# Where low parts of weights are made, and when convolution taps are queued, in a two-layer diffusion block on one Trainium2 core

## The chip, the cores and the metric

The kernel runs on one core of one Trainium2 chip. The core has TensorE (PE, matrix products; PEld is its weight load), VectorE (DVE), ScalarE (ACT), GpSimd (POOL) and SyncE (SP, which here only issues DMAs), and 16 DMA engines that move data between the chip's memory (HBM) and the core's on-chip memory (SBUF). The metric is the device time of one execution in microseconds (us); lower is better. Before the change three runs took 3119.43, 3118.53 and 3109.94 us, median 3118.53 us.

## The reference, cut to what matters

All arithmetic is float32: 1024 latent tokens and 256 context tokens, width 1024, two layers.

```python
for l in range(DEPTH):                                    # DEPTH = 2
    sh1, sc1, g1, sh2, sc2, g2 = split(silu(c) @ w_mod[l] + b_mod[l], 6)    # c_ctx likewise
    h = rms_norm(x, norm1_g[l]) * (1 + sc1) + sh1
    q, k, v, u_pool, a, b = split(h @ w_in[l])            # 4 heads, v 128 wide
    attn = softmax(q1 k1) - lam * softmax(q2 k2), times v, then rms_norm   # over ctx + latent
    pool = windows of 2, 4, 8, 16 tokens, then a 64x64 product
    conv = silu(layer_norm(depthwise_conv_31_taps(a * sigmoid(b))))
    x = x + g1 * (concat(attn, pool, conv) @ w_out[l])
    x = x + g2 * swiglu(rms_norm(x, norm2_g[l]) * (1 + sc2) + sh2)         # hidden width 2816
    # in layer 0 the context tokens pass through the same steps; they see context alone
```

## The kernel before, in words

TensorE multiplies in a rounded float32 format (fp32r). To keep accuracy each operand is held as two tiles, a high part `hi` (the value rounded) and a low part `lo` (the value less `hi`), and each product is three matmuls, hi·hi, hi·lo and lo·hi. Activations live transposed, 128 channels on the partitions, in two latent blocks of 512 tokens and one context block of 256.

Weights are read tile by tile by the class `Stream`. `load_to` issues the load of a raw tile on SP's queue; `split_to` makes `hi` with an ACT copy and `lo` in one of three ways, by a letter in the tuple `lo`, which is gone through in turn: "v" is a subtraction on VectorE, "p" the same on GpSimd, and "d" is an ACT copy of minus `hi` followed by a DMA issued from GpSimd's queue that reads the same weights from HBM once more and adds them onto it (an adding DMA). `get(i)` splits up to `split_ahead` tiles beyond tile i and loads `raw_ahead` more. `ahead(raw, split)` first splits up to `split` tiles and then loads up to `raw`; where `split_to` finds a tile that is not loaded, it issues the load and the ACT copy right behind it. Raw, hi and lo tiles of 512 KB, residual tiles, attention results and many temporaries all come from one pool of 23 slots, called `big`; smaller ones from `half` and `part`. An instruction that writes a tile waits until the slot is free, and every engine and queue runs its instructions in the order in which they were written out.

That order is written by a planner in the program itself. The class `Clock` keeps a modelled time for each engine. Work off TensorE's main line is cut into steps, Python generators in named lanes, and `adv`, called after each group of matmuls, issues steps whose due time is not past the modelled time of PE. A step that ends with `yield "v"` is due one us before VectorE's modelled queue runs out; one that ends with `yield "v-"`, used by the convolution's taps alone (`taps`, one VectorE instruction for each tap), is due 0.3 us after it has run out.

The stages of a layer, with the profile's times:

- Opening (0 to 85 us): the first two modulation parts, the first norm.
- `in_proj` (85 to 371 us in layer 0, 1835 to 2062 us in layer 1): columns of w_in, then v's four weight tiles (w_v). Beside it run the taps (lanes conv0, conv1, and convc for the context in layer 0), the layer norm behind them (`conv_end`), the pooling and the norms of q and k. In layer 0 lane "ada" computes the third modulation part (g1) from 16 tiles of 256 KB, with `lo` by adding DMAs.
- `attention` (371 to 636 us with eight context units ahead; 2062 to 2265 us): all engines in a hand-made order; what is left of taps and `conv_end` is put between.
- `out_proj` for the two latent blocks (636 to 755 us, 2265 to 2385 us), eight steps of 24 matmuls for each block, then for the context (755 to 802 us, layer 0). In layer 0 lane "ada" computes the next modulation parts beside it with VectorE products (`adaln_v`), which the second norm needs.
- The feed-forward part (from 814 and 2385 us on), whose weights get their low part on GpSimd.

Of the kernel before, what the change touches and what calls it, by code (L numbers as in the profile page):

```python
# [17 lines left out]
KD = D // P  # L18
# [47 lines left out]
QK_LANES = 2  # L66
ADA_AT = 25.0
GATED = 4
V_AHEAD = {2: (1, 1), 1: (3, 2), 0: (4, 4)}
CTX_LO = ("v", "p", "p")  # L70
EARLY = 3
POOL_ENG = "v"

# [123 lines left out]
class Kern:  # L197
# [20 lines left out]

    def due(self, name):
        d = self.lanes[name][0]  # L220
        return self.clock.at[d[0]] + (0.3 if d.endswith("-") else -1.0) if isinstance(d, str) else d

    def _step(self, name):
        q = self.lanes[name]
# [39 lines left out]
    def finish(self, *names):  # L264

        while True:
            due = [(self.due(n), n) for n in (names or list(self.lanes)) if n in self.lanes]
            if not due:
                return
            if "ada" in self.lanes and any(n.startswith("norm") for _, n in due):  # L270
                due.append((self.due("ada"), "ada"))
            self._step(min(due)[1])
# [323 lines left out]
    def in_proj(self, l, st, lat, cxb, soon, opened=None):  # L596
# [53 lines left out]
        for j in range(GATED, len(COLS)):  # L650
# [4 lines left out]
            w = st.get(j, 2)  # L655
            if len(COLS) - j - 1 in V_AHEAD:
                sv.ahead(*V_AHEAD[len(COLS) - j - 1])
            outs = [self.bank() for _ in blocks]
# [476 lines left out]


    def out_stream(self, l, n, **kw):
        return Stream(self, [self.io["w_out"][l, d] for _ in range(n) for d in range(KD)], **{"raw_ahead": 1, **kw})

    def out_proj(self, st, blocks, ready, xs, x_load, gate, done, soon=None):  # L1140

# [154 lines left out]
    def run(self):  # L1296
# [161 lines left out]
        self.lane("norm1", self.norm_h([x[1] for x in xs], rs[1], scale, shift, lat[1]))  # L1458
        self.lane("norm2", norm_c())
        self.lane("small", self.lambdas(), 60.0)  # L1460
        self.lane("ada", self.adaln(0, [2], 3.0, ne=1, split_ahead=2, raw_ahead=1, lo=("d",)), ADA_AT)

        for l in range(DEPTH):
            last = l == DEPTH - 1
# [95 lines left out]
            def ctx_soon():  # L1560
                st_out.append(self.out_stream(l, 1, raw_ahead=2, split_ahead=2, lo=CTX_LO))
                st_out[1].ahead(3, 2)
# [227 lines left out]
```

## Time and profile before

| | us | share |
|---|---|---|
| profiled execution, device time | 3113.99 | |
| its span, first to last instruction | 3112.2 | |
| PE busy | 2923.8 | 94% |
| DVE busy | 1723.9 | 55% |
| ACT busy | 1076.2 | 35% |
| POOL busy | 838.0 | 27% |
| DMA, mean | 97 GB/s | |
| granted TensorE clock, mean | 0.973 of full | |

A busy PE is not PE at its peak, since matmuls are pipelined and the granted clock varies; the shares are averages over stages with different limits, so what a stage is limited by is read from that stage's own rows.

### The profile page before, as it was taken

The page shows a single profiled execution, that of the slowest core. Times are in us where ns is not written, and L with a number is a line of the kernel's source. Part 1 is how long each engine was busy: PE and PEld are TensorE (multiplying, and loading weights), DVE is VectorE, ACT ScalarE, POOL GpSimd, SP SyncE. Part 2 cuts the span into 40 slices and gives each one's busy share as a digit, 9 for nine tenths or more (in the row PEclk, how much of TensorE's full clock was granted, in tenths as well). Part 3 has the DMA queues.
Part 4 walks back from the last instruction along what each step waited for, and adds up shares of the span by engine and source line. Part 5 has one row for each costly group of instructions (what it writes and reads, how often), then busy time and mean ns, then how long its engine had stood idle before and what let it go on. Part 6 is the DMA issues. An engine that isn't in the chain of part 4 may idle for free.

```text
span 3112.2 us, 37712 instructions
## 1 busy us (share of the span) xinstructions
PE 2923.8 (94%) x14572; PEld 2406.1 (77%) x14572; DVE 1723.9 (55%) x2674; ACT 1076.2 (35%) x1851; POOL 838.0 (27%) x759
## 2 busy tenths in 40 slices
PE   7799978988799999999999979989999999999999
PEld 3587767876688888888888768878877888888887
DVE  5777788967845554444332478769955222322223
ACT  4554367733422222221222234457734111111110
POOL 0110057810223232333322100038811222112121
PEclk9899989999899999999999989999999999999999
DMA  6565642265222222221111224672252111111111
GB/s 218 138 153 135 199 145 76 86 236 201 92 80 70 74 82 81 69 81 48 41 35 34 83 81 116 166 220 62 89 183 71 52 48 48 48 48 48 48 48 54
DMA packets 143618, 302.37 MB, mean 97 GB/s; under 512 B 14544, under 2 KB 56144, under 8 KB 143440
## 3 DMA queue, kind: packets, MB, share of 16 engines
q1 hardware_dynamic: 137104, 281.09, 28.3%
q0 software_dynamic: 6336, 18.88, 3.6%
q8 instruction: 115, 1.88, 0.2%
q14 instruction: 63, 0.52, 0.1%
HBM read 250.63 MB, written 49.28 MB: 96 GB/s over the span
## 4 chain that ended last, share of the span: by engine, by line
PE 62%; DVE 8%; ACT 3%; issue 3%; DMA 2%; POOL 1%; SPq 0%; ACTq 0%; DVEq 0%; POOLq 0%
PE bank L275 60%; DVE half L163 3%; DVE big L163 2%; DVE st L163 2%; ACT half L163 1%; PE S L275 1%; DVE at L163 1%; DMA half<-in_w_mod 1%; PE bank L280 1%; DVE part L163 1%; ACT p L163 1%; ACT big L163 1%; DMA part<-MS 0%; POOL p L163 0%; ACT at L163 0%
## 5 line engine op out<-in xcount | busy, mean ns | idle before, releaser
L275 PE MATMUL bank<-part,big 128*128 128x512 f32 (+1 forms) x7536 | 1621.0, 374 | 55.1 <-DVE part L163 16.3
L275 PEld LDWEIGHTS bank<-part,big 128*128 128x128 f32 x7536 | 1317.5, 191 | 329.0 <-DVE part L163 20.7
L163 POOL TENSOR_TENSOR big<-big,big 128x1024 fp32r<-128x1024 f32 x137 | 333.0, 2447 | 1106.3 <-ACT big L163 821.3
L275 PE MATMUL bank<-half,big 128*128 128x512 f32 (+1 forms) x2640 | 573.2, 375 | 17.3 <-DVE big L163 7.1
L275 PEld LDWEIGHTS bank<-half,big 128*128 128x128 f32 x2640 | 462.9, 190 | 120.8 <-ACT half L163 14.8
L163 DVE TENSOR_TENSOR big<-big,bank 128x512 f32<-128x512 f32 (+1 forms) x130 | 83.1, 679 | 828.4 <-PE bank L275 618.2
L163 DVE SCALAR_TENSOR_TENSOR big<-bank,mod,big 128x512 f32<-128x512 f32 (+1 forms) x560 | 391.1, 737 | 135.2 <-PE bank L275 131.2
L163 ACT ACTIVATE big<-bank 128x512 f32<-128x512 f32 x88 | 48.1, 596 | 659.7 <-PE bank L275 659.6
L163 ACT CAST big<-big 128x1024 fp32r<-128x1024 f32 (+2 forms) x274 | 250.3, 937 | 44.0 <-DVE big L163 19.5
L163 POOL TENSOR_TENSOR p<-p,p 128x512 f32<-128x512 f32 (+1 forms) x200 | 221.4, 1107 | 16.7
L163 ACT ACTIVATE half<-bank,mod 128x256 f32<-128x256 f32 x160 | 76.0, 475 | 426.1 <-PE bank L275 405.7
L163 POOL TENSOR_TENSOR big<-big,half 128x256 f32<-128x256 f32 x160 | 122.5, 766 | 352.0 <-ACT half L163 352.0
L163 DVE TENSOR_REDUCE st<-S 128x1 f32<-128x1280 f32 (+1 forms) x144 | 195.9, 1363 | 10.7 <-PE S L275 10.7
L163 ACT ACTIVATE p<-S,st 128x1280 f32<-128x1280 f32 (+1 forms) x144 | 177.8, 1234 | 44.5 <-DVE st L163 40.4
L163 POOL TENSOR_SCALAR p<-p,st 128x512 f32<-128x512 f32 (+1 forms) x200 | 124.3, 622 | 241.9 <-DVE st L163 182.0
L275 PE MATMUL S<-kv,big 128*128 128x512 f32 (+1 forms) x672 | 157.3, 370 | 10.5 <-ACT p L163 9.7
L275 PEld LDWEIGHTS S<-kv,big 128*128 128x128 f32 x672 | 120.3, 191 | 37.2 <-ACT p L163 15.8
L163 DVE SCALAR_TENSOR_TENSOR big<-big,dww,big 128x1009 f32<-128x1009 f32 (+14 forms) x120 | 148.8, 1272 | 0.4
L163 DVE TENSOR_TENSOR big<-big,big 128x512 fp32r<-128x512 f32 (+4 forms) x141 | 123.8, 886 | 32.5 <-ACT big L163 31.0
L275 PE MATMUL bank<-at,kv 128*128 128x256 f32 x960 | 137.7, 290 | 0.0
L163 DVE TENSOR_TENSOR at<-bank,at 128x512 fp32r<-128x512 f32 (+1 forms) x200 | 115.8, 589 | 28.7 <-ACT at L163 24.9
L163 ACT CAST at<-bank 128x512 fp32r<-128x512 f32 (+1 forms) x200 | 99.6, 508 | 74.7 <-PE bank L280 74.3
(111 smaller groups left out, 2376.9 us busy)
## 6 DMA issues: line engine op xcount, KB each, us to landing
big<-in_w_ffn_in SPq DMA_DIRECT2D x88, 512.0 KB, 3.6
big<-in_w_mod SPq DMA_DIRECT2D x48, 512.0 KB, 3.7
big<-in_w_ffn_out SPq DMA_DIRECT2D x44, 512.0 KB, 3.5
big<-in_w_out SPq DMA_DIRECT2D x40, 512.0 KB, 5.6
half<-in_w_mod SPq DMA_DIRECT2D x64, 256.0 KB, 5.5
big<-QS SPq DMA_DIRECT2D x128, 128.0 KB, 4.7
big<-in_w_in SPq DMA_DIRECT2D x28, 512.0 KB, 4.7
big<-in_w_in POOLq DMA_DIRECT2D x20, 512.0 KB, 5.5
```

The source lines that it names most:

```text
L163: r = fn(*a, **k)
L275: self.tc.nc.tensor.matmul(out, lhsT, rhs, start=start, stop=stop)
L280: self.tc.nc.tensor.transpose(out, in_, ident)
```

## The change

Five edits. The taps become due 0.6 us before VectorE's modelled queue runs out, instead of 0.3 us after. Ahead of the last but one column of w_in, v's third weight tile is split too. The context output projection makes all low parts by adding DMAs, where it went through VectorE, GpSimd, GpSimd in turn. The latent output projections of both layers make theirs by adding DMAs, split two tiles ahead, where VectorE made them one tile ahead. The third modulation part makes its low parts on VectorE, one tile ahead, where adding DMAs made them, two ahead.

```diff
-V_AHEAD = {2: (1, 1), 1: (3, 2), 0: (4, 4)}
-CTX_LO = ("v", "p", "p")
+V_AHEAD = {2: (1, 1), 1: (3, 3), 0: (4, 4)}
+CTX_LO = ("d",)
...
     def due(self, name):
         d = self.lanes[name][0]
-        return self.clock.at[d[0]] + (0.3 if d.endswith("-") else -1.0) if isinstance(d, str) else d
+        return self.clock.at[d[0]] - (0.6 if d.endswith("-") else 1.0) if isinstance(d, str) else d
...
     def out_stream(self, l, n, **kw):
-        return Stream(self, [self.io["w_out"][l, d] for _ in range(n) for d in range(KD)], **{"raw_ahead": 1, **kw})
+        return Stream(self, [self.io["w_out"][l, d] for _ in range(n) for d in range(KD)], **{"raw_ahead": 1, "split_ahead": 2, "lo": ("d",), **kw})
...
-        self.lane("ada", self.adaln(0, [2], 3.0, ne=1, split_ahead=2, raw_ahead=1, lo=("d",)), ADA_AT)
+        self.lane("ada", self.adaln(0, [2], 3.0, ne=1, split_ahead=1, raw_ahead=1), ADA_AT)
```

The default of `lo` in `Stream` is ("v",). Of the context projection's eight low parts three were VectorE's and five GpSimd's.

## Rows read from the trace of the kernel before

**Rows 1.** The page: the span, busy time of PE, and the chain of waits by engine.

```profile
span 3112.2 us, 37712 instructions
...
PE 2923.8 (94%) x14572; PEld 2406.1 (77%) x14572; DVE 1723.9 (55%) x2674; ACT 1076.2 (35%) x1851; POOL 838.0 (27%) x759
...
PE 62%; DVE 8%; ACT 3%; issue 3%; DMA 2%; POOL 1%; SPq 0%; ACTq 0%; DVEq 0%; POOLq 0%
```

**Rows 2.** Busy time by stage: start and end, length, busy us of PE, PEld, DVE, ACT and POOL (with instructions), granted TensorE clock, DMA share, GB/s.

```profile
85.00:185.00 100.00, 84.64 (x409) 65.26 (x408) 74.65 (x112) 52.49 (x89) 18.47 (x25) 0.88 0.67 162
...
371.00:412.00 41.00, 26.49 (x108) 21.81 (x108) 25.18 (x71) 26.04 (x65) 8.82 (x14) 0.67 0.78 235
412.00:490.00 78.00, 58.11 (x352) 49.49 (x351) 67.63 (x117) 50.46 (x94) 48.31 (x56) 0.93 0.32 95
490.00:636.00 146.00, 136.85 (x934) 121.07 (x933) 133.66 (x205) 109.24 (x197) 119.96 (x138) 1.00 0.27 80
636.00:755.00 119.00, 104.53 (x468) 81.58 (x466) 81.13 (x123) 35.93 (x50) 2.67 (x1) 0.96 0.69 243
755.00:802.00 47.00, 39.99 (x257) 37.10 (x256) 41.42 (x57) 17.71 (x27) 12.91 (x5) 0.89 0.43 140
802.00:850.00 48.00, 32.06 (x156) 25.56 (x156) 40.21 (x67) 21.30 (x33) 8.56 (x4) 0.86 0.29 94
...
2265.00:2327.00 62.00, 58.56 (x281) 47.59 (x282) 28.98 (x40) 20.11 (x29) 2.67 (x3) 1.00 0.65 223
2327.00:2385.00 58.00, 58.00 (x259) 46.93 (x257) 40.00 (x56) 26.52 (x37) 7.27 (x3) 1.00 0.24 79
```

**Rows 3.** Waits of PE between 85 and 185 us: waiting engine, line, tile, what it waited for, us in total, times, longest.

```profile
PE mod L275 <- DMA half<-in_w_mod: 11.6, 7, 5.2
PE bank L275 <- DMA big<-in_w_in: 3.5, 1, 3.5
```

**Rows 4.** DMA issues between 100 and 180 us: tiles, queue, count, size, median us from issue to landing.

```profile
half<-in_w_mod POOLq DMA_DIRECT2D x16, 256.0 KB, 8.5
```

**Rows 5.** Groups between 660 and 850 us, shapes kept apart: engine, operation, tiles, shape, count, busy us, mean ns, idle before. The first is the subtraction for a `half` tile, the next two those for a `big` one on GpSimd and on VectorE.

```profile
L163 DVE TENSOR_TENSOR half<-big,half 128x512 fp32r<-128x512 f32 x2 | 1.4, 690 | 0.0
...
L163 POOL TENSOR_TENSOR big<-big,big 128x1024 fp32r<-128x1024 f32 x10 | 26.5, 2660 | 193.7 <-ACT big L163 146.2 <-DVE half L163 39.3 <-PE bank L275 8.2
L163 DVE TENSOR_TENSOR big<-big,big 128x1024 fp32r<-128x1024 f32 x16 | 19.5, 1224 | 5.9 <-ACT big L163 5.9
```

**Rows 6.** Instructions that read the tap weights: count, shortest, median and longest ns, first and last start.

```profile
L163 DVE SCALAR_TENSOR_TENSOR big<-big,dww,big x120: 1259/1272/1286, 98.8 to 2030.1; 128x1009 f32<-128x1009 f32 x8, 128x1010 f32<-128x1010 f32 x8, 128x1011 f32<-128x1011 f32 x8, 128x1012 f32<-128x1012 f32 x8
L163 DVE SCALAR_TENSOR_TENSOR big<-big,dww x60: 460/473/971, 126.4 to 452.0; 128x241 f32<-128x241 f32 x4, 128x242 f32<-128x242 f32 x4, 128x243 f32<-128x243 f32 x4, 128x244 f32<-128x244 f32 x4
```

**Rows 7.** Timeline of VectorE and ScalarE around the start of layer 0's attention: start, length, engine, line, operation, tiles, shape, count. The first is layer 0's last latent tap, the next a silu of `conv_end`, the third two of the last context taps.

```profile
354.14 1.27 DVE L163 SCALAR_TENSOR_TENSOR big<-big,dww,big 128x1009 f32<-128x1009 f32 x1
...
402.99 0.81 ACT L163 ACTIVATE big<-big,params 128x512 f32<-128x512 f32 x1
...
451.51 0.97 DVE L163 SCALAR_TENSOR_TENSOR big<-big,dww 128x242 f32<-128x242 f32 x2
```

**Rows 8.** Timeline of SP, ScalarE and PE at the end of the columns of layer 0; in brackets the idle time before and what ended it.

```profile
295.06 0.33 SPq L163 DMA_DIRECT2D big<-in_w_v  x1
...
301.78 1.04 ACT L163 CAST big<-big 128x1024 fp32r<-128x1024 f32 x1 [7.73 <-DMA big<-in_w_v]
...
304.26 1.26 PE L275 MATMUL bank<-big,pwr 128*128 128x256 f32 x3 [7.27 <-ACT big L163]
```

**Rows 9.** Waits of PE between 660 and 850 us, columns as in rows 3.

```profile
PE bank L275 <- DVE part L163: 15.8, 7, 12.3
PE bank L275 <- ACT big L163: 9.9, 5, 6.5
PE bank L275 <- POOL big L163: 6.1, 3, 2.2
```

**Rows 10.** Timeline of VectorE and GpSimd in that stretch: the same four VectorE products without and beside a GpSimd subtraction.

```profile
744.26 2.74 DVE L163 SCALAR_TENSOR_TENSOR half<-half,cond_raw,half 128x512 f32<-128x512 f32 x4
...
763.82 4.82 DVE L163 SCALAR_TENSOR_TENSOR half<-half,cond_raw,half 128x512 f32<-128x512 f32 x4
764.20 2.57 POOL L163 TENSOR_TENSOR big<-big,big 128x1024 fp32r<-128x1024 f32 x1 [14.92 <-ACT big L163]
```

**Rows 11.** DMA queues by window: packets, MB, share of the 16 engines' time. The first two are for 118 to 148 us (q0 holds the adding DMAs, q1 SP's), the third for 640 to 720 us.

```profile
q0 software_dynamic: 1301, 3.17, 58.4%
q1 hardware_dynamic: 1809, 4.46, 43.7%
...
q1 hardware_dynamic: 10802, 23.82, 82.8%
```

**Rows 12.** The page's DMA issues: the adding DMAs of w_in, size and median us from issue to landing.

```profile
big<-in_w_in POOLq DMA_DIRECT2D x20, 512.0 KB, 5.5
```

**Rows 13.** Timeline at the start of layer 1's output projection: the subtraction of the first weight tile on VectorE, the first matmuls, and those that waited for a load of the mixed tokens.

```profile
2270.58 1.83 DVE L163 TENSOR_TENSOR big<-big,big 128x1024 fp32r<-128x1024 f32 x2 [0.25 <-ACT big L163]
...
2272.50 1.56 PE L275 MATMUL bank<-big,big 128*128 128x512 f32 x6
...
2277.21 0.72 PE L275 MATMUL bank<-part,big 128*128 128x512 f32 x2 [1.29 <-DMA part<-MS]
```

## The prediction

> **What bounds the kernel now.** I read the page's summary and its chain of waits first: PE is busy for 94% of the span and is 62% of the chain, VectorE is 8%, DMA 2% [rows 1]. So time is to be had only where PE stands still, or where its clock is down. The busy times by stage show where that is [rows 2]: PE lacks 15 us in 85–185, 14.5 in 371–412, 20 in 412–490, 14.5 in 636–755, 7 in 755–802 and 16 in 802–850, but next to nothing in layer 1's output projection (3.4 us in 2265–2327, none in 2327–2385). Third come the waits of these stretches by releaser, fourth the timelines around single waits, last the DMA queues by window, since two edits move work between VectorE and the DMA engines. What can't be measured against no change here is about 0.3%, 9 us.
>
> The sum is made against the profiled execution, 3113.99 us (span 3112.2, so 1.8 us lie around it). The median of the three runs is 4.5 us above it, and it lies inside their spread of 9.5.
>
> **A. Third modulation part: 16 low parts from adding DMAs to VectorE.** In 85–185 PE waits seven times, 11.6 us in all, for the adding DMAs of these tiles, and once 3.5 us for one of w_in [rows 3]. One such landing takes 8.5 us [rows 4]. Removed: 16 adding DMAs of 256 KB and 16 ACT copies. Added: 16 subtractions of 0.69 us [rows 5], 11.0 us on VectorE, which is idle for 25 us of this stretch [rows 2]; that idle time covers them, but norm, taps and pooling stand in the same queue, and if the cover fails 11 us of their work come later. Gain at most 11.6 + 3.5 = 15; at least 0, since VectorE then waits on the loads as the adding DMA did, and splitting one tile ahead instead of two leaves less room. I take half, **−8** (0 to −15).
>
> **B. Taps due 0.9 us earlier.** A step now comes before VectorE's modelled queue has run dry, not after. 120 latent taps take 1.27 us and 60 context taps 0.47 [rows 6]. No work is added; a gap of up to 0.9 us ahead of a tap can close. Work queued behind a tap on VectorE (splits, norms of q and k) comes up to one tap later; PE waits for that where the split is late. What would be gained is seen at the start of layer 0's attention: the last latent tap starts at 354.14, a silu of the layer norm behind the taps runs at 402.99, in the middle of the attention's exponentials, and the last context taps at 451.51 [rows 7]. So left-over taps and their layer norm go beside the attention, where PE is at 58.11 of 78 us in 412–490 and at 136.85 of 146 (93.7%) in 490–636 [rows 2]. At the latter share 58.11 us would take 62: 16 us. With 371–412 (PE 26.49 of 41) at the share of 412–490 (74.5%) it would take 35.5: 5.5 more. Layer 1, with no context, has a share like 490–636 and I expect nothing there. Full gain some 22, upper end 25 with the gaps themselves. At the other end a tap ahead of three or four late splits costs 1.27 each: +4. The context taps' lane has the last turn and will still end inside the attention, so I take half, **−12** (+4 to −25).
>
> **C. v's third tile ahead.** Its load is issued at 295.06, the ACT copy waits 7.73 us for it and PE 7.27 for that [rows 8]. The edit issues load and copy behind each other earlier, but the load needs a free slot of `big`, and one more slot is then taken while the last column runs. If SP has to wait for the slot, what it has behind it (loads of w_in) waits too, at worst for some 5 us (a landing, [rows 12]). **−2** (+5 to −7).
>
> **D. Layer 0's output projections, 636 to 850.** Removed from VectorE: 16 latent subtractions of 1.224 us [rows 5] and three of the context's, 23 us; from GpSimd: five of the context's, 2.66 each. Added: 24 ACT copies of about a microsecond (ACT is busy for 36 of 119 us and 18 of 47 [rows 2], so idle time hides them), and 24 adding DMAs of 512 KB.
>
> The reliefs: PE waits 15.8 us for VectorE's small tiles, 9.9 for ACT's copies and 6.1 for GpSimd's subtractions [rows 9]. The last must go, and VectorE is slowed by these too: its same four products take 2.74 us alone and 4.82 beside a GpSimd split [rows 10], 2.1 us each, five times, 10.5 us. VectorE works for 41.4 of 47 us in 755–802 and 40.2 of 48 in 802–850 [rows 2], and its modulation products, which the second norm needs, set the end there. So relief is bounded by 6.1 + 15.8 = 22 from the waits; I take 16, 6 from GpSimd's and 10 from the products that end sooner. What is late next is PE's own stream, or the load.
>
> Against it, the DMA engines. The adding DMAs of 118–148, 3.17 MB, take 58.4% of 30 us [rows 11], 17.5 us, so 512 KB take 2.9 us of all 16 engines, while SP's 4.46 MB take 43.7%, 13.1 us, or 1.54 us for 512 KB. In 640–720 SP's queue alone holds them for 82.8% of 80 us [rows 11], 66 us. About 11 adding DMAs start there, 11 × 2.9 = 32, together 98 us in 80: 18 over. Loads can slide into 720–755, where the share is lower (69% over the whole stage [rows 2], 82 us of 119, so about 16 in the last 39), and they run a tile ahead; so I take half, +9 (0 to +18). Then the first low part: it must land before the first hi·lo product, about 5 to 8 us after its copy ([rows 12, 4]), where VectorE is done with two subtractions in 1.83 and PE starts at once [rows 13]. In layer 1, PE waits there to 2277.21 anyway for mixed tokens, so about 3 us are left over; I take +3 for layer 0 as well. Also the pool of 23 slots: two tiles ahead need one more pair than one ahead, which the pool doesn't have at the last steps of the first block, so a claim then waits until PE is done with a step; ACT, standing at that claim, holds up the copies behind it. At worst PE stands for one landing there, 5.5 us, which lies within the half taken above.
> Sum −16 + 9 + 3 = **−4** (+18 to −22).
>
> The Trainium skill ("DMA: Bandwidth & Descriptors", "Anatomy of one DMA — SWDGE (gpsimd) path") fits a DMA issued by GpSimd by 2.0 us plus the bytes at 436 KB per us. By that 512 KB would occupy the engines 1.2 us instead of the rows' 2.9, the window would hold 66 + 13 = 79 of 80 us, and D's +9 would vanish (an estimate: 3084 instead of 3093). The page draws no line between copying and adding; the row of this kernel's adding DMAs decides, so I keep 2.9.
>
> **E. Layer 1's output projection, 2265 to 2385.** VectorE loses 16 subtractions (20 us), but PE was idle for only 3.4 us in it, so relief is −1. Added: the first landing +3 [rows 13], and in 2265–2327 DMA engines busy for 65% of 62 us (40) get 10 × 2.9 = 29 more, 69 in 62: at worst +7, of which I take +3. **+5** (0 to +10). From 2327 on the share was 24%, so no cost there.
>
> Sum: −8 − 12 − 2 − 4 + 5 = −21, so **3093 us**.
>
> **Rivals.**
> 1. All reliefs are cashed and the adding DMAs cost nothing: A −15, B −25, C −7, D −22 with a start of +3, E +1 (−2 of relief, +3 of start): −65, **3049**. For it: all waits named are real waits of PE, and layer 1's stage has DMA room in its second half. Against it: such waits share their causes, and what is late next takes part of it.
> 2. Slower: the adding DMAs fill the 16 engines, and PE waits for weights through both output projections. It decides from the point where loads and adding DMAs together exceed their stretch: 98 in 80 and 69 in 62 above say that they do. Price +18 +3 in layer 0, with its relief not cashed since PE then waits for DMA, +7 +3 in layer 1, with A −8, B −5 and C 0: +18, **3132**. For it: 82.8% before anything is added. Against it: loads are issued ahead and the second halves of both stages have room. The Trainium skill says the same of the place ("DMA: Bandwidth & Descriptors", "Issuing engines are not separate DMA queues": whichever engine issues, the DMAs run on the same 16 engines and interleave); rows 11 agree in that q0 and q1 shared one stretch with 58.4 + 43.7 = 102% of it.
> 3. The edits don't do what they say: taps displace as much as they gain, VectorE's split waits where the adding DMA did, and D's two sides cancel: A −4, B 0, C 0, D −2, E +2: −4, **3110**. For it: PE is 94% busy, and a planner that models time moves other steps when one moves.
>
> **How the numbers follow.** My forecast 0.50, rival 1 0.13, rival 2 0.22, rival 3 0.15. The forecast's own range is 3075 to 3106 (B at its full −25 and half of D's DMA term gone, 18 below; A and B halved and E's DMA term doubled, 13 above). Over all cases, 3062 to 3130: left out are rival 1 where it comes out in full and rival 2 where it comes out above its working, together about 0.2. Faster: forecast and rival 1, 0.63; within 0.3%: rival 3, 0.15; slower: rival 2, 0.22.
>
> **What would show it.** A: no wait of PE for in_w_mod's tiles in 85–185; wrong if VectorE's subtraction stands there with as much. B: the last latent tap well before 354, silu before 380, last context tap before 440, and attention from 412 on shorter; wrong if these starts stay. C: the wait of 7.27 at v gone. D: waits for GpSimd's tiles gone, the four products back at 2.74 everywhere, 755–850 shorter by 10 or more; against it, waits of PE on adding DMAs of w_out, and a share near 100% in 640–720. E: waits of PE at the start of 2265–2327 and a DMA share above 0.9. The forecast is wrong if the output projections take over 10 us longer than before (rival 2), or if 371–490 keeps its 119 us (rival 3).

## The result and the profile after

The changed kernel took 3160.97 us (median of 4, 3155.36 to 3166.88) against 3117.88 us before: ratio 1.0144, 95% interval 1.0117 to 1.017, **slower by 43 us**. The forecast of 3093 had the wrong sign. The page after: span, busy times, and the chain of waits by engine.

```profile
span 3153.6 us, 37800 instructions
...
PE 2932.1 (93%) x14572; PEld 2415.7 (77%) x14572; DVE 1685.1 (53%) x2655; ACT 1109.5 (35%) x1877; POOL 843.4 (27%) x778
...
PE 69%; DVE 12%; issue 9%; DMA 4%; ACT 4%; POOL 2%; SPq 1%; ACTq 0%; POOLq 0%; DVEq 0%
```

Against [rows 1] PE's busy time is up by 8.3 us and the span by 41.4, so some 33 us are standstill. Both kernels run 14572 matmuls, so their stages can be cut at equal matmul counts: the start of matmul number n in one is set beside that of number n in the other. First busy times by stretch of the kernel before, at cuts that [rows 2] lack (start and end, length, busy us and instructions of PE, PEld, DVE, ACT, POOL, granted clock, DMA share, GB/s):

```profile
185.20:304.30 119.10, 111.83 (x612) 95.74 (x610) 87.06 (x155) 55.95 (x107) 7.25 (x13) 0.98 0.51 133
304.30:371.00 66.70, 66.70 (x313) 55.44 (x314) 50.89 (x100) 23.76 (x53) 0.77 (x1) 0.95 0.61 176
...
2265.10:2385.50 120.40, 116.50 (x538) 94.42 (x537) 69.38 (x95) 47.13 (x66) 9.89 (x6) 1.00 0.45 153
```

The same view of the kernel after, cut at the same counts:

```profile
83.50:179.60 96.10, 82.13 (x409) 64.49 (x407) 77.44 (x120) 41.45 (x71) 4.68 (x9) 0.89 0.42 117
179.60:303.60 124.00, 116.21 (x612) 98.84 (x611) 90.68 (x153) 56.57 (x107) 8.06 (x13) 0.96 0.54 136
303.60:383.20 79.60, 68.30 (x314) 55.52 (x313) 66.85 (x140) 31.70 (x66) 0.00 (x0) 0.89 0.48 144
383.20:486.10 102.90, 81.87 (x458) 69.29 (x458) 77.39 (x157) 68.53 (x146) 54.58 (x69) 0.87 0.57 167
...
632.00:774.60 142.60, 113.29 (x468) 91.00 (x467) 60.81 (x107) 52.27 (x65) 15.52 (x18) 0.83 0.88 257
774.60:874.00 99.40, 71.93 (x411) 64.50 (x410) 70.58 (x122) 48.65 (x71) 16.21 (x11) 0.83 0.59 166
...
2289.30:2426.50 137.20, 119.57 (x539) 96.40 (x537) 48.52 (x79) 63.67 (x82) 23.66 (x22) 0.96 0.73 196
```

Read the lengths (the third number) against each other:

| stage (times of before) | before | after | difference | forecast |
|---|---|---|---|---|
| 85–185, opening of the columns | 100.0 | 96.1 | −3.9 | A −8 |
| 185–371, columns and v | 185.8 | 203.6 | +17.8 | C −2 |
| 371–490, first part of the attention | 119.0 | 102.9 | −16.1 | B −12 |
| 636–755, layer 0, latent projection | 119.0 | 142.6 | +23.6 | D −4, with the next row |
| 755–850, context projection and behind | 95.0 | 99.4 | +4.4 | |
| 2265–2385, layer 1's projection | 120.4 | 137.2 | +16.8 | E +5 |

The edits up to the attention's first part nearly cancel. The loss lies in the output projections. PE's waits in layer 0's two stages, from 632 to 874 us, that answer to [rows 9]:

```profile
PE bank L275 <- DMA big<-in_w_out: 31.1, 8, 6.6
PE bank L275 <- ACT big L163: 14.7, 3, 9.4
PE bank L280 <- DVE mod L163: 6.6, 1, 6.6
PE bank L275 <- DVE part L163: 3.8, 3, 3.4
PE bank L275 <- POOL big L163: 0.6, 1, 0.6
```

Of the waits for VectorE's small tiles (15.8) 3.8 us are left, of those for GpSimd's subtractions (6.1) 0.6, as forecast, and 31.1 us on the adding DMAs stand in their place. In layer 1's projection it is 15.6 us, four times. The timeline of the engines in layer 1 shows how one of these waits comes about (start, length, engine, operation; in brackets the idle time before and its releaser):

```profile
2331.10 0.75 DVE L163 SCALAR_TENSOR_TENSOR big<-bank,mod,big 128x512 f32<-128x512 f32 x1 [3.42 <-PE bank L275]
2332.40 0.32 SPq L163 DMA_DIRECT2D big<-XD  x1
...
2344.39 0.75 DVE L163 SCALAR_TENSOR_TENSOR big<-bank,mod,big 128x512 f32<-128x512 f32 x1 [11.14 <-DMA big<-XD]
...
2345.17 0.63 ACT L163 ACTIVATE half<-big 128x512 f32<-128x512 f32 x1 [10.62 <-DVE big L163]
...
2345.71 1.03 ACT L163 CAST big<-big 128x1024 fp32r<-128x1024 f32 x1
...
2346.77 1.06 ACT L163 ACTIVATE big<-big 128x1024 fp32r<-128x1024 f32 x1
...
2348.13 0.86 POOL L163 DMA_DIRECT2D big<-in_w_out  x1 [12.44 <-DMA big<-in_w_out]
...
2353.34 1.79 PE L275 MATMUL bank<-big,big 128*128 128x512 f32 x4 [3.33 <-DMA big<-in_w_out]
```

VectorE adds a finished step to the residual, which here had to be loaded first (XD); ScalarE squares that sum for the norm, and only behind the square, in its queue, stand the two copies of a weight tile; GpSimd issues, and 5.2 us later PE goes on. From residual add to product it is 8.95 us here; a step of PE is 5.55. The add itself is late: the one before it ran at 2331.10, so one step later it would have come at about 2336.7, but the load of its residual, issued at 2332.40 behind eight loads of mixed tokens, landed after 11.9 us (median of the eight such loads 5.8). The 8.95 us alone would have fitted into two steps; with an add 7.7 us late they didn't.

### The profile page after: what moved, and what is told of

Read it like the earlier page. It is cut to its first block, busy times and chain, and to the rows that moved or that the text cites. A ratio compares the mean times of both kernels' runs of the same rounds, so it can differ in the third digit from the quotient of the medians.

```text
span 3153.6 us, 37800 instructions
## 1 busy us (share of the span) xinstructions
PE 2932.1 (93%) x14572; PEld 2415.7 (77%) x14572; DVE 1685.1 (53%) x2655; ACT 1109.5 (35%) x1877; POOL 843.4 (27%) x778
## 4 chain that ended last, share of the span: by engine, by line
PE 69%; DVE 12%; issue 9%; DMA 4%; ACT 4%; POOL 2%; SPq 1%; ACTq 0%; POOLq 0%; DVEq 0%
PE bank L275 64%; DVE big L163 5%; DVE st L163 4%; PE S L275 2%; DVE half L163 2%; DMA big<-in_w_out 2%; PE bank L280 1%; DVE at L163 1%; POOL p L163 1%; ACT p L163 1%; ACT half L163 1%; PE mod L275 1%; ACT big L163 1%; SPq L163 1%; POOL big L163 1%
## 5 line engine op out<-in xcount | busy, mean ns | idle before, releaser
L275 PEld LDWEIGHTS bank<-half,big 128*128 128x128 f32 x2640 | 461.6, 190 | 122.9 <-ACT half L163 15.8
L163 POOL TENSOR_TENSOR big<-big,big 128x1024 fp32r<-128x1024 f32 x132 | 319.8, 2439 | 868.0 <-ACT big L163 656.8
L163 DVE TENSOR_REDUCE st<-S 128x1 f32<-128x1280 f32 (+1 forms) x144 | 195.7, 1362 | 14.1 <-PE S L275 14.1
L275 PE MATMUL bank<-big,big 128*128 128x512 f32 x480 | 126.5, 413 | 28.1 <-DMA big<-in_w_out 25.5
L163 POOL DMA_DIRECT2D big<-in_w_in x20 | 17.4, 871 | 464.2 <-ACT big L163 397.4
L275 PEld LDWEIGHTS bank<-big,big 128*128 128x128 f32 x480 | 94.2, 199 | 52.9 <-DMA big<-in_w_out 28.4
```

Source lines behind the costliest of these rows:

```text
L163: r = fn(*a, **k)
L275: self.tc.nc.tensor.matmul(out, lhsT, rhs, start=start, stop=stop)
```

## The experiments

Two theories were put against each other for the projections, and a third for a part. **Landing chain**: the work from the residual add of one step to the landing of a low part (add 0.75, square 0.63, copies 2.1, issue and landing 5.5 to 8) is about as long as the two steps, 11.1 us, in which it has to be done, so there is little room for a delay on it before PE waits. **Full engines** (rival 2 of the prediction): bytes fill the 16 DMA engines, and PE waits for weights. **Slots**: two tiles ahead take a pair of `big` that the pool lacks. Times are medians beside runs of the kernel before on the same chip (3115.62 us for the first eight, 3117.99 for the last four).

**e1_abc: the projections as before, the other edits kept.**

```diff
-... "split_ahead": 2, "lo": ("d",), **kw})
+... **kw})
-CTX_LO = ("d",)
+CTX_LO = ("v", "p", "p")
```

> The after kernel with all three output projections put back as before (low parts by VectorE, and VectorE, GpSimd, GpSimd for the context): only the taps, v and the third modulation part are changed. By the comparison of the two profiles at equal matmul counts the loss lies wholly in the output projections: about -4 us against before, 3108 to 3118. If instead the earlier edits push work into the projections, it stays above 3130.

3111.95 us, ratio 0.9986 (0.9975 to 0.9997), as expected: the loss is the projections' alone.

**e2_vec_two: VectorE's low parts, two tiles ahead.**

```diff
-... "split_ahead": 2, "lo": ("d",), **kw})
+... "split_ahead": 2, **kw})
```

> The after kernel with the latent projections' low parts on VectorE again but still split two tiles ahead; no adding DMA for them, the same number of slots taken. Theory DMA (the adding DMAs' bytes fill the 16 engines): 3110 to 3125. Rival slots (two tiles ahead take a pair that the pool lacks, SP stands at the claim with the modulation loads behind it): most of the loss stays, 3140 to 3165. Rival landing (the adding DMA lands too late for its step however idle the engines are): 3110 to 3125.

3111.62 us, ratio 0.9982 (0.9972 to 0.9992). The slots of two tiles ahead cost nothing by themselves; that theory falls. The context projection keeps its adding DMAs here, so the loss is the latent projections'.

**e3_dma_one: adding DMAs, one tile ahead.**

```diff
-... "split_ahead": 2, "lo": ("d",), **kw})
+... "split_ahead": 1, "lo": ("d",), **kw})
```

> The after kernel with the latent projections' low parts by adding DMAs, but one tile ahead: all bytes, the slots of before. Theory DMA: the loss stays, 3150 to 3170. Rival slots: the loss goes, 3110 to 3130. Rival landing: worse than after, since each low part has a step less to land in, 3170 to 3220.

3198.65 us, ratio 1.0261 (1.0246 to 1.0277): 38 us worse than the change itself with the same bytes, as only the landing theory had it. Layer 1's projection took 176.1 us against 120.4, 3.5 us more for each of 16 steps, with the same 26.84 MB moved and the engines at 0.58 (window of e3_dma_one, columns as above; the kernel after had 0.73):

```profile
2293.50:2469.60 176.10, 132.08 (x538) 104.70 (x538) 48.51 (x79) 63.73 (x82) 23.75 (x22) 0.87 0.58 152
```

**e4_dma_eighth: an eighth of the bytes.**

```diff
-self.k.nc.gpsimd.dma_start(lo, self.aps[self.n_split], accum_op=ALU.add)
+self.k.nc.gpsimd.dma_start(lo[:, 0:1, :], self.aps[self.n_split][:, 0:1, :], accum_op=ALU.add)
```

> The after kernel with each adding DMA of the output projections cut to one eighth of its tile (64 KB for 512), so seven eighths of these low parts are left as minus the high part: same issues, same waits, same slots, one eighth of the bytes. Theory DMA: the loss goes, 3110 to 3125. Rival slots: it stays, 3145 to 3165. Rival landing, if it is a fixed time: it stays, 3140 to 3160.

3115.75 us, ratio 1.0001 (0.9992 to 1.001). The loss goes, so a landing that costs the same at any size is out. But fewer bytes both land sooner and leave the engines free, so this run doesn't part the two theories. It shows something else: with most of the DMA's price taken away (PE still waits 3.8 us for one adding DMA there), layer 0's two stages take 118.4 + 91.7 us against 119 + 95. The relief of VectorE and GpSimd is worth about four us, not sixteen.

**e5_lo_last: later use of the low part.**

```diff
# shortened
+for k in order:
+    ... hi[:, k, :] with blk.hi[k], hi[:, k, :] with blk.lo[k]; self.adv()
+for k in order:
+    ... lo[:, k, :] with blk.hi[k]; self.adv()
-for k in order: all three; self.adv()
```

> The after kernel with the order of matmuls changed in the output projections alone: all products with the weights' high part first, the eight with the low part last, so that a low part has some 3.7 us more to land (two thirds of a step of 5.55). Theory landing chain (from the end of step i-1: residual add 0.75, square 0.63, two ACT copies 2.1, issue 0.9, landing 7.2, together 11.6 us, against two steps of 11.1): nearly all waits of PE for the adding DMAs go, layer 1's loss from +17 to below +5, layer 0's from +32 to below +15, time 3120 to 3140. Theory full engines (loads and adding DMAs fill the 16 engines through both stages): the same bytes take the same time, 3148 to 3165.

3127.41 us, ratio 1.0046 (1.0031 to 1.0061): about 31 of the 43 us are back with every byte still moved. Layer 0's two stages took 132.0 and 89.5 us, 7.5 more than before where the change took 28, with the engines busier than in the changed kernel (0.96 of the latent stage where that had 0.88). Layer 1 kept 13.7 us of 16.8, against the expectation. 9.9 of it are two waits: 4.12 at the start, and 5.78 behind a residual add for whose load VectorE stood 11.12 us. The planner is called at twice as many points of a step in this run; what that alone does was not tried.

**e6_unwaited_adds: all bytes, nobody waits.**

```diff
 (on e2_vec_two, layer 1 alone, behind each st.get)
+for ap in st.behind if n == 2 else ():
+    for h, t in enumerate(self.spare):
+        nc.gpsimd.dma_start(t, ap[:, 4 * h:4 * h + 4, :], accum_op=ALU.add)
```

> The kernel e2_vec_two (low parts of the latent projections on VectorE, two ahead) with the same adding DMAs issued beside it in layer 1 alone, onto two spare tiles that nothing reads (two of 256 KB for each weight tile; two slots of half fewer there). All bytes, nobody waits for them. Theory landing chain: layer 1's output projection costs at most 3 us more than in e2_vec_two, 3108 to 3120. Theory full engines: loads of weights and residuals come late, PE waits for them, 8 to 17 us more in that stage, 3120 to 3132.

3120.63 us, ratio 1.0017 (1.0006 to 1.0028), at the lower end of what the theory of full engines had, and the stage is 9.1 us longer than in e2_vec_two (122.1), which is in that theory's range too. The windows of the run show another reason (first half and second half of layer 1's projection):

```profile
2260.40:2323.90 63.50, 59.21 (x282) 47.61 (x282) 29.92 (x41) 21.20 (x31) 17.44 (x21) 1.00 0.93 272
2323.90:2391.60 67.70, 61.96 (x259) 49.51 (x257) 37.65 (x54) 26.12 (x36) 21.05 (x19) 0.92 0.65 141
```

With the engines at 0.93 the first half took 63.5 us (62.1 in the kernel before, at 0.65; 63.7 in e2_vec_two). The second lost 9.4, and its timeline names another cause: GpSimd's queue stood at the spare tiles' DMAs, and the first split of the feed-forward weights behind them.

```profile
2366.45 0.86 POOL L163 DMA_DIRECT2D spare<-in_w_out  x1 [3.91 <-DMA spare<-in_w_out]
2367.73 0.86 POOL L163 DMA_DIRECT2D spare<-in_w_out  x1 [0.42 <-DMA spare<-in_w_out]
2368.29 5.12 POOL L163 TENSOR_TENSOR big<-big,big 128x1024 fp32r<-128x1024 f32 x2
...
2371.01 6.87 PE L275 MATMUL bank<-part,big 128*128 128x512 f32 x19 [5.25 <-POOL big L163]
```

PE's wait of 5.25 us and, at a granted clock of 0.92, 4.0 us of slower matmuls (61.96 us busy against 57.95 in e2_vec_two) make up the second half's loss. So the excess over the landing theory's figure is the experiment's own making. In layer 0 this wasn't tried.

**e10_last_two_vec: e5_lo_last, and the first two low parts of each latent projection on VectorE.**

```diff
-"lo": ("d",), **kw})
+"lo": ("v", "v") + ("d",) * 14, **kw})
```

> The kernel e5_lo_last with the first two low parts of each latent projection on VectorE, the other fourteen by adding DMAs. If what e5_lo_last still loses at the start of the two projections is the first landing, queued behind the loads issued with it, layer 1's start (8 us in after, 6 in e5_lo_last) goes to below 2 and layer 0 gains 1 to 3: 3112 to 3121. If the start's wait is for the raw loads themselves, it stays: 3124 to 3130.

3117.0 us, ratio 0.9998 (0.9987 to 1.0008), as expected if it is the first landing. 36 of 40 adding DMAs are left, and the time is that of the kernel before; the three stages of the projections take 6.2 us more than before, where the change took 44.8. The latent projection of layer 0 at equal counts:

```profile
634.60:757.30 122.70, 104.71 (x469) 83.58 (x468) 64.45 (x113) 51.90 (x65) 13.79 (x16) 0.92 0.97 290
```

The DMA engines are busy for 97% of it, more than in the changed kernel, and it takes 3.7 us more than before where the change took 23.6. Full engines by themselves don't stop PE. The first landing of a projection, behind the loads issued with it, was half of what e5_lo_last still lost in layer 1: 134.1 us became 127.0, and the start has no wait for an adding DMA. Layer 0's two stages gained 7.9 us, more than the 1 to 3 that were expected; why so much stays open. Of the 6.6 us that are left, 3.56 are a wait behind a late residual again (VectorE stood 10.43 us for its load). So the two theories meet: loads in a full stretch come late and delay the chain, and how much room the chain has decides whether PE waits. How much of the change's loss began with such a delay wasn't measured.

**The edits ahead of the projections.** On the kernel before:

```diff
 e7_taps_v:      taps due -0.6, V_AHEAD 1: (3, 3)
 e8_taps_mid:    taps due -0.3
 e9_mid_v:       taps due -0.3, V_AHEAD 1: (3, 3)
 e11_taps_early: taps due -0.5
 e12_taps_late:  taps due -0.1
```

> The kernel before with the taps' due time and v's third tile alone (third modulation part by adding DMAs, all projections as before). If the third modulation part on VectorE is what gains 4 to 5 us in 85 to 185, that gain is absent at equal matmul counts and the loss of 17 us between 236 and 330 us stays, since it comes from taps ahead of splits: 3112 to 3122. If the loss came from the modulation part's subtractions on VectorE, it goes here: 3095 to 3105.

> The kernel before with the taps due 0.3 us before VectorE's modelled queue runs out (before: 0.3 after; after: 0.6 before) and nothing else. If the loss in the columns and the gain in the attention are two sides of the same taps, both are there in part and the sum stays within 6 us of before: 3109 to 3121. If they are independent, the smaller lead keeps the gain of 16 and loses less: 3098 to 3108.

> The kernel e8_taps_mid with v's third tile split ahead too: that edit alone. If the edit is what its wait says (PE's 7.3 us at v in the kernel before, already gone in e8_taps_mid, where PE waits 1.9), nothing is left to gain: 3088 to 3097. If its slot held through the last columns is what puts the loss of 17 us there in e7_taps_v, the time rises: 3100 to 3112.

> The kernel before with the taps due 0.5 us before VectorE's modelled queue runs out, nothing else. Theory: the lead decides how many taps stand ahead of the products that PE waits for in the columns; close to 0.6, the waits of e7_taps_v (some 12 us) come back and eat the gain: 3103 to 3113. Rival: the loss in e7_taps_v comes from v's third tile and not from the lead: 3085 to 3097.

> The kernel before with the taps due 0.1 us before VectorE's modelled queue runs out, nothing else. Theory: already here the gap ahead of each tap closes, most of the gain of e8_taps_mid is there: 3090 to 3102. If the gain grows with the lead, it is a third of that: 3104 to 3112.

The last two columns are the lengths of two stages at equal matmul counts, named by their times in the kernel before.

| run | us | ratio to before (95%) | 304–371, us | 371–490, us |
|---|---|---|---|---|
| (before) | | | 66.7 | 119.0 |
| (after) | 3160.97 | 1.0144 (1.0117 to 1.017) | 79.6 | 102.9 |
| e7_taps_v | 3107.73 | 0.9975 (0.9965 to 0.9984) | 78.2 | 103.5 |
| e8_taps_mid | 3092.07 | 0.9931 (0.9914 to 0.9948) | 63.2 | 107.6 |
| e9_mid_v | 3101.35 | 0.994 (0.992 to 0.996) | 78.0 | 108.7 |
| e11_taps_early | 3111.44 | 0.9984 (0.9969 to 1.0) | 76.5 | 107.1 |
| e12_taps_late | 3095.04 | 0.992 (0.9902 to 0.9939) | 65.4 | 106.6 |

e7_taps_v came out between its two expectations; its stage of 304–371 is as long as in the changed kernel, so that loss isn't the modulation part's. e8_taps_mid, one number changed, beats both kernels by more than its interval: 23.6 us under before, better than both of its expectations had it. It keeps most of the attention's gain and pays nothing for it in the columns, so the columns' loss isn't the price of the attention's gain. The gain in time is there at −0.1 already and mostly gone at −0.5, as the theory of e11 and e12 had it. For e9_mid_v the medians say 9 us and the intervals of the ratios overlap; the profile is clearer, 14.8 us more in one stretch, and names the place; the time is in the range that was given for a slot held too long. Timeline of e9_mid_v, VectorE and PE:

```profile
300.98 0.44 DVE L163 TENSOR_TENSOR big<-big 128x271 f32<-128x271 f32 x1 [11.00 <-PE bank L275]
...
314.33 0.98 PE L275 MATMUL bank<-groups,big 128*128 128x4 f32 x4 [10.58 <-DVE big L163]
```

VectorE's first pooling sum, which reads and writes `big` tiles alone, stands for 11 us until PE is done with a tile; it is read here as the claim of a `big` slot. Behind it stand the squares for the norms of q and k, and PE's sums over them wait 10.58 us. The kernel after shows the same pair at 307.89 and 321.24, and a second wait at 254.68, which e1_abc has too and e7_taps_v, with the same lead but without A, has not:

```profile
254.68 0.98 PE L275 MATMUL bank<-groups,big 128*128 128x4 f32 x4 [6.13 <-DVE big L163]
...
307.89 0.44 DVE L163 TENSOR_TENSOR big<-big 128x271 f32<-128x271 f32 x1 [9.70 <-PE bank L275]
...
321.24 0.99 PE L275 MATMUL bank<-groups,big 128*128 128x4 f32 x4 [9.17 <-DVE big L163]
```

That e11_taps_early, without v's edit, also waits there (6.4 us at 309) says that the lead alone can bring it too. How it does that, tap by tap, stays open.

## Why the prediction was wrong

**D failed, in both of its main terms.** "Sum −16 + 9 + 3": the reliefs of 16 are worth about 4 (e4_dma_eighth). The waits on VectorE and GpSimd were real, but behind them stood others: PE's waits between 632 and 850 us add up to 37.7 us before and still to 30.9 in e4_dma_eighth. A part of the 16 was also misread: of the four products that take 4.82 us beside GpSimd [rows 10] one takes 2.83 and the others 0.75 each, and such a product comes three times up to 815 us, some 6 us and not 10.5. And the DMA term priced the wrong thing. The occupation was right: between 632 and 760 us the queues' rows are

```profile
q1 hardware_dynamic: 11968, 26.22, 56.1%
q0 software_dynamic: 2033, 7.41, 31.7%
```

which is 40.6 us for 14.1 adding DMAs, 2.87 us each, against 2.9 in the working. But an overbooked stretch isn't what PE waits for; at 97% it lost 3.7 us. What was missing is the chain behind VectorE's residual add: the working set a landing (5 to 8 us) against VectorE's 1.83 for the projection's start alone, and for all other steps took two tiles ahead as room enough, but for a claim of a slot. The landing's median was 7.8 us between 632 and 760 us, and add, square and two copies stand ahead of the issue. The claim of a slot came too: ScalarE stood 9.93 us for a tile of PE's until 703.55, the adding DMA issued behind it at 704.90 landed 8.7 us later, and PE waited 3.95 for it. Where −4 was forecast for layer 0, 636–850 lost 28, the relief of 4 included.

A part of it was in no term at all: behind such waits TensorE's granted clock was down. Two stretches of the kernel after, before and behind PE's standstills of 2.6 and 5.8 us at 682 to 692 us, columns as above:

```profile
668.40:685.00 16.60, 14.10 (x61) 11.09 (x59) 6.45 (x11) 1.52 (x2) 0.00 (x0) 0.99 1.05 357
692.10:698.50 6.40, 6.38 (x23) 5.71 (x24) 0.69 (x1) 1.52 (x3) 0.86 (x1) 0.50 0.51 82
```

(The DMA share is the sum of the packets' times, so it can come out above 1.) The granted clock goes from 0.99, the level of 2.4 GHz, to 0.50, that of 1.2. Over the whole latent projection of layer 0 it was 0.83 against 0.96, and PE was busy for 113.3 us with the 468 matmuls that took 104.5 before: 8.8 of the 23.6 us are slower matmuls, not waits.

**E failed by the same term.** +3 for the start was 8.1: PE waits 9.03 us there, since the first two low parts landed after 10.2 and 10.5 us, not 5 to 8, and the wait for mixed tokens that was to hide most of it is 1.9 us in the trace before, not the whole time to 2277.21. +3 for the rest was 8.7; 16.8 against 5.

**B** was right in mechanism and in its gain: the last latent tap went from 354.14 to 330.9, the last context tap from 452 to 385.8, and 371–490 is shorter by 16.1 (forecast: 16 to 22 in full). Its price was named ("splits, norms of q and k come up to one tap later") and mis-sized: not +4 for three or four late taps, but waits of 6 to 9 us, since what PE needs is several instructions back in VectorE's queue.

**C** removed its wait of 7.27, and so nearly does B alone: e8_taps_mid without C has 1.9 us of such waits. Its price was put at SP's claim of a slot, at worst +5; it came at VectorE's, some 10.

**A**'s stage is shorter by 3.9 us where 8 was forecast, and 1.8 of these come without A too (98.2 us in e7_taps_v). The wait on in_w_mod's DMA is gone, but 6.6 us on ScalarE's tiles stand there now (0.3 before), and the wait on w_in's DMA is 6.1 us instead of 3.5. Against e7_taps_v, e1_abc has no gain by A: medians 3111.95 and 3107.73. What was gained is lost again further down the columns, at 254.68 among others. A, B and C together were forecast at −22 and came to −3.7 (e1_abc).

**The rivals.** Rival 2 had the direction, and its 3132 was nearer than the forecast; its mechanism by itself was not the right one. Its point of decision was 98 us of engine time in 80; in 640–720 the engines were at 0.90 in the kernel after, and in e10_last_two_vec at 1.01, which did little harm by itself.

The Trainium skill ("DMA: Bandwidth & Descriptors", "Issuing engines are not separate DMA queues") has it that the DMAs of all issuing engines interleave on the same 16. The runs agree: the same adding DMAs landed in 5.5 us at the end of layer 1's projection in e3_dma_one (median of four between 2410 and 2460 us), and in 7.8 among the loads of layer 0 in the kernel after. The page's inference that issuing from several saves only issue time is about bytes; what decided here is what was queued ahead of the issue.

## What to carry to other kernels

Before moving work from an engine to a DMA, write down the chain from the event that lets it be issued to its landing, queue by queue, and set it against the steps that it has; a share of the engines near one is no loss while that chain is short enough, and a low share is no comfort when it isn't. A wait that goes is worth the distance to the next one, not its own length. A small lead on a queue can be worth more than the edits around it: try it alone, and at more than one value.

## What the runs showed that was not expected

- An adding DMA of 512 KB holds the 16 engines for 2.87 us and a plain load of that size for 1.44 (71.8 us for 26.22 MB by the rows above), twice as long. Its landing has a median of 5.5 us where little else moves (e3_dma_one, as above), while the Trainium skill ("DMA: Bandwidth & Descriptors", "Anatomy of one DMA — SWDGE (gpsimd) path") gives a fit of 2.0 us plus the bytes at 436 KB per us, 3.2 us for this size (an estimate by that page). The fit doesn't hold for adding DMAs here; the measured figure decides.
- In 122.7 us with the DMA engines at 97%, PE was as fast as before to within 3.7 us.
- VectorE's waits can be for `big` slots: 11 us at a pooling sum that names PE as its releaser.
- A residual load that lands late (11.9 us for a median of 5.8) shows two steps further on as PE's wait for an adding DMA; the wait names the last link of the chain, not the one that was late.
